# Hybrid attention and retention step: where three kinds of loads stand ahead of the output projection, and which half of a row block is turned first

## The chip, the cores and the metric

The kernel runs on one core of one Trainium2 chip. The metric is the device time in microseconds (us) of one execution. Several runs of the kernel are timed and their median is taken; one further execution is recorded by the hardware profiler, and all rows shown below come from that one.

## The reference, cut to what matters

One layer of a decoder with two groups of heads. 1024 prompt tokens and 32 sample tokens (8 sequences of 4) go through an input projection, a sparse softmax attention (A), a retention (B), and then through the part that this change is about, which the reference calls the merge:

```python
def _merge(x, oa, ob, ga, gb, p, w_out, g_post, w_ple_up, w_ple_gate):
    ya = silu(ga) * oa                        # attention, 512 columns
    yb = silu(gb) * head_norm(ob)             # retention, 512 columns
    y = concat([ya, yb]) @ w_out              # output projection, 1024 x 1024
    x = x + rmsnorm(y, g_post)                # post-norm with the weights g_post
    ple = p @ w_ple_up                        # the per-layer embedding, 256 -> 1024
    gate = sigmoid(x @ w_ple_gate)            # 1024 x 1024
    return x + ple * gate
```

All arrays are float32. The outputs are the new x of prompt and sample tokens, the new keys and values, and the retention's states.

## The kernel before, in words

**Products in three passes.** Every large product is done in a reduced-precision float32 format (F32R in the code), with each operand split into a high part and a low part: high times high, high times low, low times high. In the output projection these are the lines L262, L263 and L264 (`mm_a`): one row block of 128 tokens against 256 columns takes 8 slices of the contraction, three matmuls each, so 24 matmuls. Slices 0 to 3 belong to the attention's half of a row, slices 4 to 7 to the retention's half. The three matmuls of a slice, and the slices, run in order within a row block.

**Weights.** `load_w` (L173 to L177) brings 256 columns of a weight matrix in two halves of 512 rows through two buffers called `wraw`. ScalarE casts a half to the high part (L176), GpSimd subtracts to get the low part (L177). The 32 sample tokens use the raw weights directly (`mm_s`, L271), so a `wraw` buffer is free for the next column block only when the sample tokens' matmuls have read it.

**Attention phase.** It runs over 8 query blocks `qb`; SyncE's queue loads the queries of the next block (L1507) and the gates (L1536). Between the prompt's steps the sample tokens' attention is threaded in; GpSimd gathers its keys and values (L1144). Its last results go to `oaT` (L1379 and L1594), and from there to `ysT` (L1640), the left operand of `mm_s`. The attention's result of the prompt stands in `yaT`, 16 KB in each partition.

**The output projection's begin.** For each of the 8 row blocks `tb`, `split_T` makes the left operands `yTh` and `yTl`. The attention's half comes from `yaT`: a cast on ScalarE (L1619), a subtraction on GpSimd (L1620). The retention's half is loaded from DRAM as `yb` (three buffers, L1638), turned by four TensorE transposes into a PSUM bank called `pty` (L1624), cast on ScalarE (L1626), and subtracted on VectorE (L1627).

**The projection's loop.** Four column blocks `cb` of 256 columns; in each, eight row blocks and the sample tokens (called block 8), each into one of four PSUM banks. `take_y` empties a bank: ScalarE squares it for the norm (L1663), VectorE multiplies it by `gpost`, the post-norm weights spread over all partitions (L1664). While `cb` is 2, `load_p` brings the embedding's input `p` as `pv` (L1699), and ScalarE and VectorE split it (L1701, L1702). While `cb` is 3, `finish_y` completes the norm and turns the rows for the gate. Then come four column blocks of the gate (L262 to L264 into `pg`) and the embedding (`pu`), whose weights `load_up` brings (L1731).

**What sets the order.** Nothing is written out by hand: the program is traced in its textual order, and a scheduler fixes each engine's order of instructions at compile time by a simulated timeline, where earlier text has priority and an instruction that could start earlier may be pulled ahead. At run time each engine works through its fixed list, and waits at the head of the list when something is not ready. SyncE issues nearly all loads and stores, in one list.

**Memory.** Tiles of a later phase may stand where tiles of an earlier one stood; they wait for those to be released. In the compiled kernel before, `yaT` has the bytes 212960 to 229343 of each partition, and `gpost` the bytes 217056 to 221151, so `gpost` lies inside `yaT`. The pools on the right side are stacked from the top downwards.

## Time and profile before

| | |
|---|---|
| median of 3 runs | 1083.84 us (1078.32 to 1085.11) |
| the profiled execution's own time | 1081.17 us |
| its span, first to last instruction | 1079.4 us |
| time outside the span | 1.8 us |
| mean granted TensorE clock | 0.97 of full speed |
| TensorE matmul (PE) busy | 999.9 us, 93% of the span |
| VectorE (DVE) busy | 698.3 us, 65% |
| ScalarE (ACT) busy | 507.2 us, 47% |
| GpSimd (POOL) busy | 287.9 us, 27% |

How to read the rows: a row of the timeline has the start in us, the duration in us, the engine, the line of the program, the operation, what it writes and reads, and how many instructions the row merges; in brackets the idle time of the engine before it and what ended that. PEld is TensorE's loading of its stationary operand, SPq is SyncE's issue of a transfer. In a table by stretches each engine has its busy time and the number of instructions, then come the granted TensorE clock (1.00 is full speed), the mean busy share of the 16 DMA engines, and GB/s. A row of the waits has who waited for whom, the total in us, how often, and the longest. The chain of waits is followed back from the last instruction: each row is what the work then hung on.

### The profile page before, as it was taken

How to read it: one execution, taken by the hardware profiler on the slowest of the kernel's cores; microseconds unless marked ns; L12 is line 12 of the kernel's file. 1: busy time of each engine (PE TensorE's matmuls, PEld its weight loads, DVE VectorE, ACT ScalarE, POOL GpSimd, SP SyncE). 2: the span in 40 equal slices, each digit the busy share in tenths (PEclk: the TensorE clock that was granted, in tenths of full speed). 3: DMA queues.
4: the chain of work that ended last, by engine and by line, in shares of the span. 5: the costliest groups of instructions: out<-in, count | busy, mean ns of one | idle time of the engine just before them, and what ended most of it. 6: DMA issues, size and time to landing. Idle time of an engine off the chain costs nothing.

```text
span 1079.4 us, 19681 instructions
## 1 busy us (share of the span) xinstructions
PE 999.9 (93%) x7375; PEld 844.5 (78%) x7375; DVE 698.3 (65%) x2012; ACT 507.2 (47%) x1094; POOL 287.9 (27%) x287
## 2 busy tenths in 40 slices
PE   3899997988999889999889996999998799999998
PEld 2899997666776788898788884566665799999998
DVE  6847768989401898978967947776763522684332
ACT  5545554986434256842523436655554332452210
POOL 3102223111201532413713521635331321122100
PEclk9999999999999889999989995999999899999999
DMA  8211235546443211202201624524211511332211
GB/s 284 67 59 50 78 95 178 173 137 204 127 158 120 58 40 39 66 18 87 71 12 42 179 85 118 148 79 118 60 45 51 154 60 40 116 126 80 89 37 41
DMA packets 98309, 102.24 MB, mean 95 GB/s; under 512 B 21347, under 2 KB 88387, under 8 KB 95907
## 3 DMA queue, kind: packets, MB, share of 16 engines
q1 hardware_dynamic: 92450, 74.74, 23.1%
q0 software_dynamic: 5760, 26.22, 7.9%
q8 instruction: 58, 0.95, 0.4%
q14 instruction: 41, 0.33, 0.1%
HBM read 79.25 MB, written 21.68 MB: 94 GB/s over the span
## 4 chain that ended last, share of the span: by engine, by line
PE 65%; DVE 13%; issue 7%; ACT 6%; DMA 6%; POOL 3%; SPq 1%; DVEq 0%; POOLq 0%; ACTq 0%
PE pb L252 4%; PE pb L253 4%; PE pb L254 4%; PE pg L262 3%; PE pg L264 3%; PE pg L263 3%; PE po L262 2%; PE po L264 2%; PE po L263 2%; PE pvg L263 2%; PE pvg L264 2%; PE pvg L262 2%; PE ob L1577 2%; PE pox L808 2%; PE ptp L1569 2%
## 5 line engine op out<-in xcount | busy, mean ns | idle before, releaser
L1144 POOL DMA_INDIRECT kvs<-in_cache_kv,idx x64 | 66.1, 1032 | 92.0 <-ACT pT L1574 29.8
L262 PE MATMUL pqk<-whi_qkb,xh 128*128 128x256 f32 x256 | 75.7, 296 | 3.7 <-DVE rp L1033 3.7
L262 PE MATMUL po<-whi_o,yTh 128*128 128x256 f32 x256 | 74.0, 290 | 4.7 <-DVE x L1664 4.1
L262 PE MATMUL pvg<-whi_vgb,xh 128*128 128x256 f32 x256 | 76.6, 299 | 1.2 <-ACT sg L1046 1.1
L263 PE MATMUL pvg<-wlo_vgb,xh 128*128 128x256 f32 x256 | 75.9, 297 | 0.0
L264 PE MATMUL pvg<-whi_vgb,xl 128*128 128x256 f32 x256 | 74.6, 291 | 0.0
L263 PE MATMUL pqk<-wlo_qkb,xh 128*128 128x256 f32 x256 | 74.5, 291 | 0.0
L264 PE MATMUL pqk<-whi_qkb,xl 128*128 128x256 f32 x256 | 74.1, 289 | 0.0
L264 PE MATMUL po<-whi_o,yTl 128*128 128x256 f32 x256 | 73.3, 288 | 0.0
L263 PE MATMUL po<-wlo_o,yTh 128*128 128x256 f32 x256 | 73.1, 286 | 0.0
L262 PE MATMUL pg<-whi_g,yTh 128*128 128x256 f32 x256 | 72.7, 284 | 0.0
L264 PE MATMUL pg<-whi_g,yTl 128*128 128x256 f32 x256 | 72.3, 282 | 0.0
L263 PE MATMUL pg<-wlo_g,yTh 128*128 128x256 f32 x256 | 72.3, 282 | 0.0
L497 DVE SCALAR_TENSOR_TENSOR score<-r,wi,score 128x384 f32<-128x384 f32 (+5 forms) x42 | 44.3, 1054 | 21.0 <-ACT r L493 19.8
L1562 ACT ACTIVATE L<-L,mn 128x128 f32<-128x128 f32 (+7 forms) x64 | 49.5, 776 | 14.1 <-DVE mn L1559 13.9
L262 PEld LDWEIGHTS pqk<-whi_qkb,xh 128*128 128x128 f32 x256 | 49.3, 193 | 7.9 <-issue 5.0
L262 PEld LDWEIGHTS po<-whi_o,yTh 128*128 128x128 f32 x256 | 49.8, 194 | 6.4 <-DVE x L1664 4.3
L1758 DVE TENSOR_TENSOR sgm<-pu,sgm 128x256 f32<-128x256 f32 x32 | 13.6, 424 | 62.3 <-PE pu L264 55.3
L262 PEld LDWEIGHTS pvg<-whi_vgb,xh 128*128 128x128 f32 x256 | 49.7, 194 | 3.1 <-ACT sg L1046 1.3
L1569 PEld LDWEIGHTS ptp<-cst,L 128*128 128x128 f32 x288 | 31.9, 142 | 24.3 <-issue 19.6
L493 ACT ACTIVATE r<-si 128x384 f32<-128x384 f32 (+5 forms) x48 | 36.3, 759 | 30.2 <-PE si L351 29.0
L264 PEld LDWEIGHTS pqk<-whi_qkb,xl 128*128 128x128 f32 x256 | 49.5, 194 | 1.1 <-issue 0.8
(540 smaller groups left out, 3288.0 us busy)
## 6 DMA issues: line engine op xcount, KB each, us to landing
wraw_qkb<-in_w_in SPq DMA_DIRECT2D x16, 256.0 KB
wraw_vgb<-in_w_in SPq DMA_DIRECT2D x16, 256.0 KB
wraw_o<-in_w_out SPq DMA_DIRECT2D x8, 512.0 KB
qas<-qas_d SPq DMA_DIRECT2D x8, 512.0 KB
xr<-in_x_prompt SPq DMA_DIRECT2D x8, 512.0 KB
wraw_g<-in_w_ple_gate SPq DMA_DIRECT2D x8, 512.0 KB
out_y_prompt<-sgm SPq DMA_DIRECT2D x32, 128.0 KB
qas_d<-qst SPq DMA_DIRECT2D x8, 384.0 KB
```

The source lines that it names most:

```text
L252: nc.tensor.matmul(pt[:m, :n], wh, xh[:, k, ts], start=(k == 0), stop=False)
L253: nc.tensor.matmul(pt[:m, :n], wh, xl[:, k, ts], start=False, stop=False)
L254: nc.tensor.matmul(pt[:m, :n], wl, xh[:, k, ts], start=False, stop=(k == KC - 1))
L262: nc.tensor.matmul(pt[:, :n], ah, hi[:, k, :n], start=(k == 0), stop=False)
L263: nc.tensor.matmul(pt[:, :n], ah, lo[:, k, :n], start=False, stop=False)
L264: nc.tensor.matmul(pt[:, :n], al, hi[:, k, :n], start=False, stop=(k == kc - 1))
L493: nc.scalar.activation(r[:, :n], s[:, :n], AF.Relu)
L497: nc.vector.scalar_tensor_tensor(sc, r[:, :n], wi[:, qb, h:h + 1], sc, op0=ALU.mult, op1=ALU.add)
L808: nc.tensor.matmul(po[u2 * 64:u2 * 64 + 64, :], qbd[:, b, :], kT[:, u2 * 512:u2 * 512 + 512], start=True, stop=True)
L1144: return nc.gpsimd.indirect_dma_start(out=dst, out_offset=None, in_=kvflat, in_offset=bass.IndirectOffsetOnAxis(ap=idx, axis=0))
L1562: behind[0] = nc.scalar.activation(L[:, :n], L[:, :n], AF.Exp, bias=least, scale=-1.0, accum_out=sm[:, i4:i4 + 1])
L1569: nc.tensor.transpose(tp[:, i4 * 128:i4 * 128 + 128], P[i4][:, kb * 128:kb * 128 + 128], ident)
```

## The change

- `gpost` gets a pool of its own at the top of the right side, opened ahead of `yaT`, so that it stands beside `yaT` and not inside it; the other pools of the attention on the right side move down by 4096 bytes. It is loaded during the attention, in the query block `qb` 3, behind the load of the queries for block 4 (`issue_after` orders an instruction behind another one in the same engine's list).
- The loads of the embedding's input (`pv`) and of its weights (`wur`) are ordered behind the last weight load that was traced before them (`last_w`). For `pv` that is the second half of the projection's fourth column block, for the first `wur` the second half of the gate's first column block.
- `split_T` treats the retention's half of a row block first, then the attention's half, where it has both.
- In the first column block the sample tokens' product stands behind row block 3 instead of behind row block 2.

```diff
@@ load_w
+                last_w[0] = nc.sync.dma_start(raw[:, :, c:c + w], ...).ins
-                nc.sync.dma_start(raw[:, :, c:c + w], ...)
@@ ahead of yaT
+    gpp = ctx.enter_context(pool("gpp", side="right"))
+    gpost = gpp.tile([128, D], F32, name="gpost")
     yas = ExitStack()
     yap = yas.enter_context(pool("yap", side="right"))
     yaT = yap.tile([128, 4, T], F32, name="yaT")
@@ load_q
-        nc.sync.dma_start(q.bitcast(F32), qas_d[:, :, qb * 128:(qb + 1) * 128])
+        last_q[0] = nc.sync.dma_start(q.bitcast(F32), qas_d[:, :, qb * 128:(qb + 1) * 128]).ins
@@ for qb in range(8)
             qnext = load_q(qb + 1)
+            if qb == 3:
+                with tc.issue_after(last_q[0]):
+                    nc.sync.dma_start(gpost, I["g_post"].to_broadcast([128, D]))
@@ split_T
-        for a in range(2):
+        for a in (1, 0) if first is not None else range(2):
@@ behind the row blocks' split
-    gpost = mr.tile([128, D], F32, name="gpost")
-    nc.sync.dma_start(gpost, I["g_post"].to_broadcast([128, D]))
@@ load_p
-        nc.sync.dma_start(pv, src)
+        with tc.issue_after(last_w[0]):
+            nc.sync.dma_start(pv, src)
@@ for cb in range(4)
-        for tb in (8, *range(8)) if cb else (0, 1, 2, 8, 3, 4, 5, 6, 7):
+        for tb in (8, *range(8)) if cb else (0, 1, 2, 3, 8, 4, 5, 6, 7):
@@ load_up
-        nc.sync.dma_start(raw, w_up[:, cb * 256:(cb + 1) * 256].rearrange("(k p) c -> p k c", p=128))
+        with tc.issue_after(last_w[0]):
+            nc.sync.dma_start(raw, w_up[:, cb * 256:(cb + 1) * 256].rearrange("(k p) c -> p k c", p=128))
```

## The prediction, written before the change was run

> **What bounds the kernel now.** The page first: which engine is full. Then the stages of the output projection and what follows it, as a table by stretches.

> ```profile
> PE 999.9 (93%) x7375; PEld 844.5 (78%) x7375; DVE 698.3 (65%) x2012; ACT 507.2 (47%) x1094; POOL 287.9 (27%) x287
> ...
> 833.50:873.10 39.60, 31.80 (x248) 29.40 (x252) 20.18 (x36) 16.66 (x44) 16.15 (x11) 0.91 0.40 119
> 873.10:921.50 48.40, 48.40 (x419) 46.97 (x419) 10.13 (x24) 13.22 (x42) 9.52 (x4) 1.00 0.14 45
> 921.50:955.00 33.50, 32.12 (x289) 30.42 (x289) 28.13 (x90) 15.81 (x47) 4.82 (x2) 1.00 0.45 143
> 955.00:1079.40 124.40, 120.77 (x1035) 117.84 (x1033) 49.01 (x100) 27.97 (x59) 18.61 (x9) 1.00 0.20 67
> ```

> The rows are column block 0, blocks 1 and 2, block 3, and the gate. From 873.1 to the end TensorE is busy without a hole but for 1.4 us in block 3 and the last results. So a microsecond that TensorE gains ahead of 873 comes off the end one for one, as long as the weights keep up. Block 0 is the exception: 39.6 us, 31.8 busy, clock 0.91. TensorE's waits from there on name the 7.8 us:

> ```profile
> PE po L262 <- DVE x L1664: 4.1, 1, 4.1
> PE po L271 <- DVE ysT L1640: 2.3, 1, 2.3
> PE ptxs L1683 <- DVE rz_y L237: 1.4, 1, 1.4
> PE pty L1624 <- DMA yb<-yb_d: 1.3, 3, 0.6
> ```

> (1.4 is block 3's.) The chain of waits says what stood behind the longest:

> ```profile
> 846.07 1.47 DVE pTl L1702
> 847.56 0.37 SPq L1699
> ...
> 847.98 6.32 DMA gpost<-in_g_post
> ...
> 854.32 0.44 DVE x L1664
> ...
> 854.80 0.58 PE po L262
> 855.38 0.21 PE po L263
> ```

> SyncE issued `gpost` at 847.98, after a `pv` that waited for VectorE; it landed after 6.32 us; only then could VectorE empty a PSUM bank, and TensorE get the bank for row block 3. The DMA engines' share of the stretch, 0.40 against 0.14 in the next, is the crowd in front of it.

> The wait has a second price, the clock:

> ```profile
> 835.22:838.64 3.42, 1.61 (x17) 1.20 (x18) 1.72 (x2) 1.87 (x4) 3.42 (x4) 1.00 0.00 0
> 848.88:852.29 3.41, 1.34 (x11) 0.96 (x9) 0.90 (x2) 0.65 (x3) 0.00 (x0) 1.00 0.66 186
> 852.29:855.70 3.41, 0.90 (x4) 0.90 (x5) 1.80 (x5) 1.22 (x5) 0.00 (x0) 0.50 1.06 269
> 855.70:859.11 3.41, 3.41 (x19) 3.41 (x18) 0.73 (x2) 0.41 (x1) 0.00 (x0) 0.50 0.33 110
> ...
> 858.38 0.96 PE L1624 MATMUL pty<-cst,yb 128*128 128x128 f32 x4
> 859.09 0.38 PE L263 MATMUL po<-wlo_o,yTh 128*128 128x256 f32 x1
> ...
> 859.98 0.28 PE L262 MATMUL po<-whi_o,yTh 128*128 128x256 f32 x1
> 860.10 0.28 PE L263 MATMUL po<-wlo_o,yTh 128*128 128x256 f32 x1
> ```

> At half clock a matmul follows the last after 0.21 us, at full clock after 0.12 (859.98 to 860.10). A stretch of 3.4 us with 1.34 us of matmul was followed by half clock for 6.8 us; one with 1.61 us was not.

> **The change part by part.**

> *`gpost` early.* Its bytes lay inside `yaT`, so it could not land before `yaT` was read out, wherever it stood in SyncE's list; beside `yaT` it can. The load itself is the same, one issue of some 0.5 us. Gone: 4.14 us of wait (1). Also the half clock behind it (2): the 17 matmuls from 854.80 to 858.38 took 3.58 us and would take 17 x 0.12 = 2.04, and the four transposes from 858.38 to 859.09 took 0.71 and would take half; together 1.90 us. What is late next for the bank is ScalarE's square and VectorE's product, 0.4 us each, and the reading out of `yaT` for row blocks 1 and 2, whose `x2` tiles now lie in `yaT`'s bytes:

> ```profile
> 833.10 10.39 POOL L1620 TENSOR_TENSOR yTl<-yaT,yTh 128x512 fp32r<-128x512 f32 x8 [19.47 <-ACT yTh L1619]
> 833.25 1.39 DVE L1379 COPY oaT<-oT 64x8 f32<-64x8 f32 x8
> 834.68 1.08 DVE L1594 TENSOR_TENSOR oaT<-oaT,gaT 128x128 f32<-128x128 f32 x1
> 835.80 1.17 DVE L1640 COPY ysT<-oaT 128x128 f32<-128x128 f32 x1
> 834.42 0.28 PE L263 MATMUL po<-wlo_o,yTh 128*128 128x256 f32 x1
> 837.03 0.64 PE L271 MATMUL po<-wraw_o,ysT 128*32 128x256 f32 x8 [2.33 <-DVE ysT L1640]
> ```

> GpSimd is done with `yaT` at 843.5. Four banks hold four row blocks of 24 x 0.12 = 2.9 us, so the bank of row block 1 is wanted at about 833.5 + 4 x 2.9 = 845 at the earliest: covered, and without that cover it would cost what GpSimd is late.

> *Sample tokens behind row block 3.* Before, TensorE has six matmuls at 833.5 to 834.7 (high times high and high times low of three row blocks, each stopped at its low part from GpSimd) and then the sample tokens' product, which waits for VectorE's three steps until 837.0. Behind row block 3 that product is the fifth taker of four banks and cannot be pulled to this place before row block 0 is emptied. Row block 0's low part is there at 833.10 + 10.39 / 8 = 834.4, before the six matmuls end; after that GpSimd brings one per 1.3 us, and each frees 10 matmuls, 1.2 us. So of 2.33 us I take 2.0 (3); the ends are 0, if another waiting instruction stands in its place, and 2.33.

> *Retention's half first, `pv` and `wur` behind.* Three waits for `yb`, 1.33 us. `yb` was issued in between the `pv`, a `wur` and the `gpost`; without these 8 x 128 + 256 + 512 KB it lands sooner. Against it: row block 0's transposes take the bank that the sample tokens' last `oT` holds until VectorE's copies end at 834.6. I take 0.6 (4), ends -1.0 and 1.33.

> *Where `pv` goes.* Eight loads with a cast of 0.4 us on ScalarE and a subtraction of 0.4 to 1.6 us on VectorE move to blocks 2 and 3, behind the fourth block's weights:

> ```profile
> ACT pTh L1701 <- DMA pv<-in_p_T: 8.4, 4, 3.4
> ...
> 885.00:900.00 15.00, 15.00 (x133) 14.28 (x133) 3.25 (x8) 2.73 (x11) 0.00 (x0) 1.00 0.05 14
> 900.00:921.50 21.50, 21.50 (x182) 21.37 (x181) 3.51 (x9) 5.71 (x18) 4.76 (x2) 1.00 0.12 41
> ```

> There ScalarE and VectorE are about a fifth busy and the DMA engines at 0.05 to 0.12. ScalarE's waits for `pv` move too, 3.4 us at most, and the squares queue behind them; three banks in hand are 3 x 2.9 = 8.7 us. I take 0; ends -1.0 and 0. `wur` follows the gate's first weights and is used only in the gate's stretch: 0. In SyncE's list `pv` now stands behind the weights and ahead of the `xr` loads that block 3 wants.

> *`gpost`'s load in the attention.* Behind the queries of block 4. It shares the DMA engines with the gathers of the sample tokens' keys; TensorE has other work there: 0, ends -1.0 and 0.

> *The shift by 4096 bytes.* In the compiled kernel before, the first score tile `L` of the attention's second head group has the bytes 138464 to 142559, and the retention's result `acc` 132640 to 137247. Moved down by 4096, `L` lies on `acc`, and must wait until the last `acc` is stored:

> ```profile
> 620.25 2.93 DMA yb_d<-acc
> ...
> 663.10 6.50 SPq L1097 DMA_DIRECT2D yb_d<-acc  x2
> ...
> 668.97 0.28 DVE L1096 TENSOR_TENSOR acc<-acc,sgs 32x128 f32<-32x128 f32 x1 [0.48 <-ACT acc L1091]
> ...
> 669.51 0.27 DVE L1559 CUSTOM_DVE_ANT_0 L<-sa,near 128x128 f32<-128x128 f32 x1
> ```

> The last store of `acc` is issued at about 669.3; another one held its taker for 2.93 us. `L` was written at 669.51. If the store lands at once, nothing moves; with 2.93 us `L` moves to 672.2, by 2.7 us. VectorE, ScalarE's exponentials and TensorE queue behind it. The store is the sample tokens' alone, 16 KB, so I take the nearer third, -1.0 (5); ends 0 and -2.7.

> Sum: 4.14 + 1.90 + 2.0 + 0.6 - 1.0 = 7.6 us. From the profiled execution's 1081.17 that is 1073.5; that execution lies 2.7 us under the median of the runs, 1083.84, and from the median it is 1076.2. I predict the middle, **1075**.

> [...] The row: half clock began at 852.29, when TensorE had stood still for 1.6 us, after a stretch with 1.34 us of matmul in it. [...]

> **The rivals**, each from the middle of the two bases, 1082.5.

> 1. *The half clock stays* (by what another stall does): 7.6 - 1.9 = 5.7 off, 1077. For: any new hole that leaves about 1.3 us of matmul in 3.4 us brings it back. Against: none of the remaining waits is longer than 0.6 us in the sum above. 0.08.

> 2. *The first 10 us only change their waits.* Terms (3) and (4) come to nothing, since TensorE's fixed order puts transposes that wait for `oT`'s bank, or the low parts from GpSimd, where the sample product stood; and (5) takes 2.7: 4.14 + 1.90 - 2.7 = 3.3 off, 1079. For: the order is fixed ahead of time, and before it put the sample product 2.3 us too early. Against: the low parts come from GpSimd every 1.3 us from 834.4 on, which is about TensorE's own pace. 0.19.

> 3. *The second block's weights come late, and it ends slower.* The sample tokens' product frees `wraw`, and it moves back:

> ```profile
> 863.17 0.64 PE L271 MATMUL po<-wraw_o,ysT 128*32 128x256 f32 x8
> ...
> 863.87 0.38 SPq L173 DMA_DIRECT2D wraw_o<-in_w_out  x1
> ...
> 867.25 1.05 ACT L176 CAST whi_o<-wraw_o 128x1024 fp32r<-128x1024 f32 x1 [0.17 <-DMA wraw_o<-in_w_out]
> ...
> 868.38 2.40 POOL L177 TENSOR_TENSOR wlo_o<-wraw_o,whi_o 128x1024 fp32r<-128x1024 f32 x1 [21.13 <-ACT whi_o L176]
> ```

> From the product to the finished low part it is 870.8 - 863.2 = 7.6 us, and block 1 begins at 873.1. If both halves of the product are put within 7.6 us of block 0's end, TensorE waits: at worst both halves at the very end, 7.6 + 2.4 for the second subtraction = 10.0 us, and 1.9 for the half clock. 7.6 - 11.9 = -4.3: slower, 1087. Against: behind row block 3 there are four more, 11.5 us, and `yb` of the sample tokens is no longer held up. 0.06.

> 4. *All of it comes, and nothing is paid for the shift:* 4.14 + 1.90 + 2.33 + 1.33 = 9.7 off, 1073. 0.11.

> **How the numbers follow.** The forecast has 0.56, the rivals 0.08, 0.19, 0.06 and 0.11. The range: the low end is rival 4 from the fastest run shown, 1078.3 - 9.7 = 1068.6; the high end takes in rival 2 and the open ends of the small terms, 1083. Outside are most of rival 3 and some of the tails. One per cent, 10.8 us, is about what a measurement of this kernel can tell from no change; from 1083.84 that is below 1073.0 and above 1094.7. Below lie half of rival 4 and, since the bases differ by 2.7 us, some two fifths of the forecast: 0.28. Above lies none of the cases at its price, only rival 3 with more than one block's weights late: 0.04. Within: 0.68.

> **What would show it.** Right: no wait of TensorE for `x` at L1664 in block 0; clock 1.00 throughout; the sample product no longer in the first 5 us; block 0 at 30 to 33 us instead of 39.6; `pv` casts behind the fourth block's weights, and blocks 1 to 3 still full. (5) shows as VectorE's first `L` of the second head group waiting for the store of `acc`. Wrong: TensorE waiting at block 1's begin for `wraw_o` or `wlo_o` (rival 3), a row of half clock in block 0 (1), new waits on `yTl`, `pty` or `oT` of 2 us or more (2), or an attention that ends later than 833 by over 3 us.

## The result, and the profile after

The changed kernel takes 1071.88 us (median of 7 runs, 1065.73 to 1074.34) against 1083.84 for the kernel before: a ratio of **0.9901** (95% interval 0.9878 to 0.9924), 10.7 us less by the ratio (12.0 between the medians). In the later series of runs below, where the kernel before takes 1086.68 us, the ratio was 0.9901 again (0.9862 to 0.9940). The forecast was 1075; the time lies in its range, 3 us below it. That closeness hides errors of 5.0, 2.8 and 1.6 us, of both signs, as the runs below show.

The profiled execution of after is the fastest of its runs, 1065.73 us (span 1063.9). Of the 15.4 us between the two profiled executions 4.1 lie ahead of the attention, where the engines' instructions stand in the same order in both: that is the spread between runs, not the change. So the comparison goes by stages: the attention (first `sa` matmul to first `po`), column block 0 (to the sample tokens' first matmul of block 1), blocks 1 to 3 (to their first matmul of the gate), the gate (to the start of the last matmul). Tables by stretches, before and then after, the columns being length, the busy times of PE, PEld, VectorE, ScalarE and GpSimd, clock, DMA share and GB/s:

```profile
655.96:833.48 177.52, 167.45 (x1229) 107.59 (x1229) 117.97 (x438) 103.30 (x236) 65.95 (x65) 0.95 0.30 86
833.48:873.05 39.57, 31.76 (x245) 29.37 (x245) 20.20 (x36) 16.68 (x44) 16.17 (x11) 0.91 0.40 119
873.05:952.22 79.17, 77.79 (x673) 75.43 (x673) 35.48 (x104) 27.61 (x84) 14.34 (x6) 1.00 0.25 81
952.22:1075.49 123.27, 123.27 (x1065) 119.78 (x1064) 50.94 (x108) 29.39 (x63) 18.61 (x9) 1.00 0.22 71
```

```profile
651.86:825.49 173.63, 165.00 (x1229) 105.82 (x1229) 120.22 (x438) 100.46 (x233) 64.22 (x65) 0.94 0.31 90
825.49:854.86 29.37, 28.58 (x245) 27.34 (x245) 11.64 (x28) 14.11 (x35) 14.75 (x10) 1.00 0.34 106
854.86:934.38 79.52, 77.99 (x673) 75.45 (x673) 41.25 (x110) 30.30 (x93) 16.73 (x7) 1.00 0.31 97
934.38:1060.04 125.66, 123.41 (x1065) 119.75 (x1064) 53.41 (x110) 29.64 (x64) 20.47 (x9) 1.00 0.21 70
```

Block 0 is 10.2 us shorter, and its clock is full. The attention is 3.9 shorter, which the prediction had at 1 us longer. The gate is 2.4 longer, which it had at nothing. TensorE's waits in after, from block 0 to the end, show what is left (who waited for whom, total, times, longest):

```profile
PE pty L1634 <- DVE x L1684: 2.2, 1, 2.2
PE ptxs L1691 <- DVE ry_y L238: 1.1, 1, 1.1
PE pty L1634 <- issue: 0.8, 1, 0.8
PE po L265 <- DVE yaT L1598: 0.4, 1, 0.4
PE pty L1634 <- DVE ry_y L238: 0.4, 1, 0.4
```

No wait for `x` at L1672 (the old L1664), none for `ysT`, none for `yb`. (Lines of after are 3 to 10 higher than before.) The wait of 2.2 us for `x` at L1684 is new. SyncE's issues in after show the three moved loads:

```profile
683.95 0.65 SPq L1542 DMA_DIRECT2D gpost<-in_g_post  x1
...
880.79 17.66 SPq L1708 DMA_DIRECT2D pv<-in_p_T  x8
904.04 0.93 SPq L175 DMA_DIRECT2D wraw_g<-in_w_ple_gate  x2
905.02 0.50 SPq L1741 DMA_DIRECT2D wur<-in_w_ple_up  x1
```

### The profile page after: what moved, and what is told of

It is laid out like the page before. It is cut to its first block, busy times and chain, and to the rows that moved or that the text cites. A ratio compares the mean times of both kernels' runs of the same rounds, so it can differ in the third digit from the quotient of the medians.

```text
span 1063.9 us, 19686 instructions
## 1 busy us (share of the span) xinstructions
PE 991.7 (93%) x7375; PEld 838.6 (79%) x7375; DVE 699.8 (66%) x2012; ACT 504.2 (47%) x1092; POOL 288.1 (27%) x287
## 4 chain that ended last, share of the span: by engine, by line
PE 53%; DVE 8%; ACT 2%; DMA 2%; issue 1%; POOL 1%; SPq 0%; DVEq 0%; ACTq 0%; POOLq 0%
PE ob L1587 4%; PE ptp L1579 4%; PE pg L265 3%; PE pg L267 3%; PE pg L266 3%; PE po L265 3%; PE po L266 2%; PE po L267 2%; PE pvg L265 2%; PE pvg L266 2%; PE pvg L267 2%; PE sa L1563 2%; PE sa L1564 2%; PE pqk L265 2%; PE pqk L266 1%; PE pqk L267 1%
## 5 line engine op out<-in xcount | busy, mean ns | idle before, releaser
L1147 POOL DMA_INDIRECT kvs<-in_cache_kv,idx x64 | 63.6, 994 | 84.1 <-ACT pT L1584 44.7
L1572 ACT ACTIVATE L<-L,mn 128x128 f32<-128x128 f32 (+7 forms) x64 | 49.5, 775 | 13.7 <-DVE mn L1569 13.6
L266 PEld LDWEIGHTS pvg<-wlo_vgb,xh 128*128 128x128 f32 x256 | 50.7, 198 | 0.5
L267 PEld LDWEIGHTS pvg<-whi_vgb,xl 128*128 128x128 f32 x256 | 50.6, 198 | 0.6
```

The source lines that it names most:

```text
L266: nc.tensor.matmul(pt[:, :n], ah, lo[:, k, :n], start=False, stop=False)
L267: nc.tensor.matmul(pt[:, :n], al, hi[:, k, :n], start=False, stop=(k == kc - 1))
L1147: return nc.gpsimd.indirect_dma_start(out=dst, out_offset=None, in_=kvflat, in_offset=bass.IndirectOffsetOnAxis(ap=idx, axis=0))
L1572: behind[0] = nc.scalar.activation(L[:, :n], L[:, :n], AF.Exp, bias=least, scale=-1.0, accum_out=sm[:, i4:i4 + 1])
```

## The experiments

**The theory** that these tables led to had three parts: the 4096 bytes change the attention's order, and that makes it shorter; block 0 gains by `gpost` and by the begin's new order, each for its own wait; and the gate loses by `wur` being late. Its rivals: the attention's difference is chance; the queue alone carries block 0. Times are on one chip for each group of runs; the stage lengths come from one profiled execution of each kernel, between the borders above. "Old" and "new" are the two orders that the attention has in the compiled kernels: in the four profiles of the old order every engine goes through the same list of instructions, in the ten of the new through another one, and the two part at TensorE's 13th matmul.

| kernel | attention | block 0 | blocks 1-3 | gate | ratio to before |
|---|---|---|---|---|---|
| before | old 177.5 | 39.6 | 79.2 | 123.3 | |
| before_again | old 183.5 | 40.3 | 80.8 | 124.3 | |
| queue_only | old 183.5 | 34.1 | 79.0 | 126.6 | 0.9986 (0.9964 to 1.0007) |
| rest_only | old 185.8 | 30.7 | 79.6 | 128.2 | 0.9956 (0.9935 to 0.9978) |
| shift_only | new 178.1 | 39.1 | 79.4 | 124.6 | 0.9951 (0.9928 to 0.9973) |
| gpost_only | new 178.0 | 34.1 | 81.0 | 124.3 | 0.9934 (0.9908 to 0.9960) |
| gpost_pv | new 179.4 | 33.0 | 80.7 | 123.3 | 0.9911 (0.9884 to 0.9937) |
| no_queue | new 178.0 | 30.8 | 80.9 | 124.7 | 0.9894 (0.9862 to 0.9926) |
| no_halves | new 180.3 | 28.9 | 80.8 | 123.6 | 0.9879 (0.9846 to 0.9913) |
| pv_queued | new 181.6 | 29.4 | 79.3 | 124.3 | 0.9864 (0.9830 to 0.9898) |
| old_halves | new 179.5 | 28.9 | 79.6 | 125.4 | 0.9877 (0.9843 to 0.9911) |
| old_sample | new 179.6 | 29.4 | 78.9 | 126.5 | 0.9877 (0.9845 to 0.9909) |
| after | new 173.6 | 29.4 | 79.5 | 125.7 | 0.9901 (0.9878 to 0.9924) |
| after_again | new 177.8 | 29.4 | 80.0 | 128.4 | 0.9901 (0.9862 to 0.9940) |

### The shift alone

```diff
+    gpp = ctx.enter_context(pool("gpp", side="right"))
+    gpad = gpp.tile([128, D], F32, name="gpad")
+    nc.gpsimd.memset(gpad[:, 0:1], 0.0)
     yas = ExitStack()
     yap = yas.enter_context(pool("yap", side="right"))
```

> The kernel before with 4096 unused bytes ahead of yaT's pool, nothing else: gpost is loaded in its old place, block 0 begins as before. The trace of after holds ScalarE's table loads at 16 where before has 18, and its attention (first sa of the first query block to the first matmul of the output projection) takes 173.6 us where before takes 177.5. Theory: the order that the 4096 bytes force (the samples' normalisation ahead of the first exponentials) is the cause, so this kernel shows the short attention too: 16 table loads, 173 to 175 us from first sa to first po, none of the three waits for the gathered keys (1.6 us before); block 0 as before, 38 to 41 us with gpost's wait in it; time 3 to 4 us below before, ratio 0.9965. Rival A, the prediction's term (5): the shift costs 1 us, ratio 1.001, attention 178 to 179. Rival B: the two attentions differ from run to run or by gpost's load in it: attention 177 to 178, ratio 1.000.

The bytes of `gpad` are not used. This kernel has the new order, so the 4096 bytes cause it. By the time the theory holds: 0.9951, 4.5 us between the medians, and the prediction's own term, 1 us slower, is outside the interval. By the stage it does not: 178.1 us is what the rivals said (178 to 179 and 177 to 178), and the 173.6 of after was luck. Both are true if the old order takes longer than 177.5 us in other runs, so the kernel before was profiled once more:

> The kernel before once more, for a second look at its attention. Its first profile has 177.5 us from first sa to first po, as the kernels with the shifted order have (178.0, 178.0, 178.0, and 173.6 in after), yet by the times the shift alone is 0.5% faster. Theory (the old order has more holes and falls into half clock more easily): this attention is longer than 178.5 us, as the one other kernel with the old order showed (185.8). Rival: 177 to 178 us, and the shift's gain lies elsewhere or is none.

183.5 us, and the two other kernels with the old order show 183.5 and 185.8. The mean of the four is 182.6 us, that of the ten profiles with the new order 178.6 (173.6 to 181.6). The difference, 4.0 us, is near that of shift_only's time, 4.5 (1083.03 against 1087.52). The two sets of profiles overlap, so the time is the firmer of the two.

What changed in the order shows in ScalarE's timeline. Before loads an activation table three times around the first exponentials:

```profile
662.56 1.28 ACT L1562 ACT_TABLE_LOAD   x1
663.86 0.40 ACT L1562 ACTIVATE L<-L,mn 128x128 f32<-128x128 f32 x1
...
665.53 1.28 ACT L1081 ACT_TABLE_LOAD   x1
666.82 0.20 ACT L1081 ACTIVATE gy<-gv 32x2 f32<-32x2 f32 x1
...
668.95 1.28 ACT L1562 ACT_TABLE_LOAD   x1
```

In after the samples' normalisation (`gy`) and the last product into `acc` stand ahead of the first `L`. (That the scheduler does so because `L` has to wait for the bytes of `acc` is argued, not shown.)

```profile
658.48 0.20 ACT L1084 ACTIVATE gy<-gv 32x2 f32<-32x2 f32 x1
659.82 0.77 ACT L1094 ACTIVATE acc<-acc,gz,gy 32x64 f32<-32x64 f32 x2 [1.15 <-DVE gz L1090]
661.31 1.28 ACT L1572 ACT_TABLE_LOAD   x1 [0.72 <-DVE mn L1569]
662.61 0.40 ACT L1572 ACTIVATE L<-L,mn 128x128 f32<-128x128 f32 x1
```

Two loads fewer, 2 x 1.28 = 2.56 us of ScalarE. Over the whole span it is 18 of them in before and 16 in after, of 1283 ns each.

But the loads that fell away aren't the gain. Here is TensorE alone, before and then after, cut where the ninth `ob` matmul starts; the columns are length, busy time, clock, DMA share and GB/s:

```profile
655.96:679.99 24.03, 16.87 (x89) 0.61 0.35 98
679.99:833.48 153.49, 150.58 (x1141) 1.00 0.30 84
```

```profile
651.86:675.97 24.11, 15.90 (x89) 0.60 0.34 98
675.97:825.49 149.52, 149.10 (x1141) 1.00 0.30 88
```

The table loads that differ all lie in the first stretch, and it isn't shorter. In it the new order has a longer wait of TensorE for VectorE's `mn`, again before and then after:

```profile
659.70 0.47 PE L1553 MATMUL sa<-kahi,qas 128*128 128x128 f32 x1 [2.20 <-DVE mn L1559]
```

```profile
661.29 0.48 PE L1563 MATMUL sa<-kahi,qas 128*128 128x128 f32 x1 [7.89 <-DVE mn L1569]
```

And yet both orders have done the same number of matmuls when the stretch ends, 23.7 to 24.2 us after the first `sa` in all fourteen profiles. The whole difference arises after that.

Part of that shows in the clock. All profiles begin the attention with half clock (0.50) until 17 to 20 us after the first `sa` (18.8 in before, 19.4 in after). More half clock follows, from 10 to 14 us later on, in three of the four profiles with the old order (6.8, 6.8 and 10.2 us of it, 3.4 of the last another 48 us on) and in four of the ten with the new (3.4, 3.4, 3.4 and 6.8). The stretches around it in queue_only (length, busy times, clock, DMA share, GB/s), and TensorE's wait inside:

```profile
679.97:683.38 3.41, 1.55 (x11) 1.05 (x9) 0.50 (x4) 0.71 (x2) 2.31 (x3) 1.00 0.72 223
683.38:686.79 3.41, 1.08 (x4) 0.67 (x6) 2.21 (x12) 2.25 (x6) 1.10 (x2) 0.50 0.13 38
686.79:690.21 3.42, 3.42 (x18) 1.87 (x18) 2.66 (x9) 0.72 (x4) 0.79 (x1) 0.50 0.26 77
```

```profile
682.86 0.33 PE L1324 MATMUL pkg<-cst,kvs 128*128 128x128 f32 x1 [1.67 <-issue]
685.71 0.66 PE L1556 MATMUL sa<-kahi,qas 128*128 128x384 f32 x1 [2.53 <-DVE mn L1562]
```

From the granted 0.50 the estimate is that half clock for 6.8 us costs up to 3.4; in block 0 the same 245 matmuls kept TensorE busy for 31.76 us with 6.8 us of it (before) and for 28.58 without (after). Averaged, that is 3.0 us in the old order (23.8 / 4 / 2) and 0.9 in the new (17.0 / 10 / 2): at most some 2 of the 4 us. TensorE's waits behind the ninth `ob` are 4.8 us on average in the old order and 3.5 in the new, 1.2 more; in after there are none, which is its luck, and before has 2.2. Why the new order waits less there is not shown.

### gpost alone, the rest alone

gpost_only takes the pool `gpp`, `last_q` and the early load from the change, nothing else. rest_only takes all of the change but these.

```diff
# rest_only against after
-    gpp = ctx.enter_context(pool("gpp", side="right"))
-    gpost = gpp.tile([128, D], F32, name="gpost")
...
-            if qb == 3:
-                with tc.issue_after(last_q[0]):
-                    nc.sync.dma_start(gpost, I["g_post"].to_broadcast([128, D]))
...
+    gpost = mr.tile([128, D], F32, name="gpost")
+    nc.sync.dma_start(gpost, I["g_post"].to_broadcast([128, D]))
```

> Only the first part of the change: gpost in a pool of its own, loaded behind the fourth block's queries; embedding's loads, the halves' order and the sample tokens' place as before. Theory: it has the short attention (173 to 175 us) and loses gpost's 4.1 us and the half clock behind it (1.9), but keeps the waits for ysT (2.3) and yb (1.3): block 0 33 to 35 us instead of 39.6, clock 1.00 in it, nothing lost in the gate; 9 to 10 us below before, ratio 0.991. Rival: the crowd of pv loads in front of the bank matters more than gpost, and block 0 stays at 37 us or more; 4 to 5 us below before, ratio 0.996.

> The change without its first part: gpost in yaT's bytes and in its old place, the rest (embedding's loads behind the last weights', retention's halves first, sample tokens behind row block 3) as after. Theory: attention as before, 177 to 178 us with 18 table loads; gpost still has to wait until yaT is read out, at about 10 us into block 0, and lands some 2 to 3 us later, since the loads in front of it are gone: a wait for x of 1 to 4 us stays in block 0, which takes 32 to 37 us; the gate's begin loses 2.7 us as in after; in sum 0 to 5 us below before, ratio 0.9975. Rival: the queue's order is the whole gain of block 0: 29.4 us as in after, ratio 0.993.

The first came as the theory said in block 0, 34.1 us, but for the clock: behind the wait for `ysT` it was half for 3.4 us, and for 3.4 more in block 3, which may be why the time, 0.9934, gained less. The second came near its rival in block 0: 30.7 us. Alone, `gpost` brings 5.5 us of block 0's 10.2, the rest 8.9; together 10.2, not 14.4. **The parts remove the same wait.** TensorE's waits in block 0 of rest_only:

```profile
PE po L274 <- DVE x L1669: 1.2, 1, 1.2
PE pty L1629 <- issue: 0.8, 1, 0.8
PE po L265 <- DVE yaT L1593: 0.5, 1, 0.5
```

`gpost` comes from its old place, issued 13.1 us into block 0 (14.5 before), and yet the wait for `x` is down from 4.1 to 1.2 us: the first row block is emptied 17.5 us into block 0 instead of 20.8. Of its 8.9 us the time shows 4.8 (1082.75 against 1087.52); its gate is longer, 128.2 us against 123.3.

### The queue

```diff
# queue_only against before
+    last_w = [None]
...
-                nc.sync.dma_start(raw[:, :, c:c + w], ...)
+                last_w[0] = nc.sync.dma_start(raw[:, :, c:c + w], ...).ins
...
+        with tc.issue_after(last_w[0]):
             nc.sync.dma_start(pv, src)
...
+        with tc.issue_after(last_w[0]):
             nc.sync.dma_start(raw, w_up[...])
```

> Before with only pv and wur put behind the last weights; gpost in its old place, the halves' order and the sample tokens' place as before. Theory: the crowd ahead of gpost was most of its wait, so this part alone takes block 0 from 39.6 to 33 to 35 us: the wait for x falls from 4.1 to 1 to 2 us with no half clock behind it, while the wait for ysT (2.3 us) stays, because the product still stands among the first matmuls; the gate loses 2 to 4 us as in after; attention of the old order, 177 to 186 us. Ratio 0.9975. Rival: gpost still lands late, since it cannot be issued before yaT is read out, and block 0 stays at 37 us or more, ratio 1.001.

Block 0 34.1 us as the theory has it, but not as it came there. TensorE's waits in block 0 of queue_only are these two only:

```profile
PE po L274 <- DVE ysT L1643: 2.3, 1, 2.3
PE po L265 <- DVE yaT L1591: 0.5, 1, 0.5
```

With `gpost` where it always was, nothing waits for it: SyncE issues it 12.0 us into block 0 (849.59) instead of 14.5 (847.98 before), and the first row block is emptied at 853.6. The half clock of block 0 stands now behind the wait for `ysT` (840 to 847). The longer gate, 126.6 us, takes 3.3 of the 5.5 us back, and by the time alone no gain is shown: the interval of 0.9986 takes in 1.

> The change without its second part: pv and wur free to be issued early, the rest as after. Theory: with gpost landed in the attention and the halves turned, the early loads hold nobody up: short attention (173 to 175 us), block 0 29 to 31.5 us, and the gate's order is that of before, without after's waits of 2.2 and 1.1 us there; 12 to 14 us below before, ratio 0.988, some 2 us faster than the whole change. Rival: the early pv, with casts and subtractions among the begin's work, cost what the change took them away for: a wait for yb or for a bank of 2 us or more, block 0 32 us or more, ratio 0.991 or above.

no_queue takes `issue_after` away from `pv` and `wur` in the change. Block 0 is 30.8, as the theory has it, but with a wait for `yb` of 1.3 us, and the ratio lies between the theory and the rival. So the queue's part is worth 1.5 us of block 0 where the other parts are there, and 5.5 where they are not. At 0.9894 the whole is about what the change is, not 2 us faster.

### The begin's order

```diff
# old_halves, and with it no_halves and gpost_pv
-        for a in (1, 0) if first is not None else range(2):
+        for a in range(2):
# old_sample, and with it gpost_pv
-        for tb in (8, *range(8)) if cb else (0, 1, 2, 3, 8, 4, 5, 6, 7):
+        for tb in (8, *range(8)) if cb else (0, 1, 2, 8, 3, 4, 5, 6, 7):
```

> The whole change, but with each row block's attention half handled first and the retention half second, as before. Theory (the prediction's term 4): with embedding's loads gone from the front of the queue, yb is there in time in either order, and the order of the halves is worth 0 to 1 us: block 0 29 to 30.5 us, ratio 0.990. Rival: the transposes are TensorE's only work while GpSimd brings the first low parts, and without them at the front TensorE waits for yTl: block 0 31 us or more, ratio 0.992.

> The whole change, but with the sample tokens' product behind row block 2 as before. Theory (the prediction's term 3): the product stands where it waits for VectorE's ysT, or holds a bank that the next row block wants; block 0 31 to 32 us instead of 29.4, with a wait for ysT of up to 2.4 us or of one for a bank; ratio 0.9915. Rival: once the transposes of retention's half stand among the first matmuls, the product behind row block 2 finds ysT done: block 0 29.4 to 30 us, ratio 0.990.

Each undone alone costs nothing: 28.9 and 29.4 us. For old_sample that is the rival, against the theory. Undone together:

> Before with two things only: gpost early in its own pool, and pv (not wur) behind the last weights; halves and sample tokens as before. Undoing either the halves' order or the sample tokens' place cost nothing (block 0 28.9 and 29.4 us); here both are undone. Theory: one of them is needed, because with both undone the product stands among the first matmuls again and waits 2.3 us for ysT: block 0 31.5 to 33.5 us, ratio 0.990. Rival: neither is needed: 29 to 30 us, ratio 0.987.

33.0 us; one of the two is needed. The waits in block 0 of gpost_pv:

```profile
PE po L274 <- DVE ysT L1650: 2.4, 1, 2.4
PE po L265 <- DVE yaT L1598: 0.4, 1, 0.4
```

Against no_halves, which differs only in the sample tokens' place, that is 33.0 - 28.9 = 4.1 us: the wait for `ysT`, 2.4, and 1.7 by the half clock of 3.4 us behind it (TensorE busy for 30.57 us against 28.87). Turning retention's half first costs 0.5 us by comparison (pv_queued 29.4, no_halves 28.9): no_halves has no wait for `pty` at all, after has one of 0.8.

### The gate

> The whole change, but for wur, which is free to be issued early as before; only pv stands behind the last weights. Theory: after's lost time in the gate (TensorE's waits of 2.2, 1.1 and 0.4 us at its begin, gate 125.7 us from its first matmul to the last against 123.3 before) comes from wur being ready late and in an order of VectorE's that puts two gated sums ahead of the last row block's residual; with wur early the gate has the order of before: 123.3 to 125 us, while block 0 keeps after's 29.4 to 30 us. 1 to 2 us faster than the whole change, ratio 0.988. Rival: wur's load and its cast crowd block 0's begin as pv's did: block 0 30.8 us or more and nothing is gained, ratio 0.990 or above.

The gate is 124.3 us, block 0 29.4: as expected. Over all profiles the gate splits by `wur` alone: 125.4 to 128.4 us in the six profiles in which `wur` stands behind the last weights, 123.3 to 124.7 in the eight in which it does not; means 126.8 and 124.0. (Two of the six, those of rest_only and after_again, have 3.4 us of half clock in the gate, which costs some 1.8: TensorE is busy there for 125.20 us in after_again, and for 123.41 in after.) Part of this comes back one stage earlier: five of the eight have 3.4 us of half clock in block 3, and none of the six, so that blocks 1 to 3 take 80.3 us on average in the eight and 79.4 in the six. With both stages a late `wur` costs 1.9 us. VectorE's timeline at the gate's begin in after, and TensorE's wait:

```profile
942.27 1.58 DVE L1768 TENSOR_TENSOR sgm<-sh_u,sgm 32x256 f32<-32x256 f32 x1
943.78 0.14 DVE L242 TENSOR_TENSOR ry_y<-ry_y,rz_y 128x1 f32<-128x1 f32 x1
943.85 2.95 DVE L1769 TENSOR_TENSOR sgm<-sgm,x 128x256 f32<-128x256 f32 x2
946.73 1.27 DVE L1684 SCALAR_TENSOR_TENSOR x<-x,ry_y,xr 128x1024 f32<-128x1024 f32 x1
```

```profile
948.14 1.06 PE L1634 MATMUL pty<-cst,x 128*128 128x128 f32 x8 [2.25 <-DVE x L1684]
```

The last row block's residual `x` stands behind a product and two sums of the gate, and TensorE's transposes wait for it. In before it stands ahead of them, and the same sample-token product takes 0.41 us instead of 1.58 (see VectorE beside GpSimd at the end):

```profile
958.33 1.29 DVE L1676 SCALAR_TENSOR_TENSOR x<-x,ry_y,xr 128x1024 f32<-128x1024 f32 x1
...
966.06 0.41 DVE L1758 TENSOR_TENSOR sgm<-sh_u,sgm 32x256 f32<-32x256 f32 x1
```

Why the scheduler orders them so when `wur` comes late was not tried.

### Put together

no_halves is the change without the halves' turn, with only `pv` behind the last weights; after_again ran beside it.

> The combination that the runs point to: gpost early, pv (not wur) behind the last weights, sample tokens behind row block 3, the halves' order as before. Expected: block 0 28.9 to 29.4 us, gate 123.3 to 124.5 us instead of after's 125.7, attention 173 to 181 us; ratio 0.9865, 2 us faster than the whole change. Rival: the two do not add up, the gate loses the 2 us again and the ratio is 0.990.

> The whole change once more, on the chip of the runs above and for a second profile of its attention. Theory: ratio 0.988 to 0.991 as at first; attention nearer to the 178 to 181 us of the other kernels with the same order than to the 173.6 us of its first profile; block 0 29.4, gate 125.4 to 126.5 us with the waits of 2.2 and 1.1 us at its begin. Rival: the whole change's attention has something that the others lack: 173 to 175 us again.

1073.41 us against 1077.33 for the whole change on the same chip. Block 0 and gate are as expected (28.9 and 123.6). The ratios to before, 0.9879 and 0.9901, have intervals that overlap, so that it is faster isn't shown by the times. By the stages it gains 0.5 us in block 0 and 2 to 5 in the gate, and loses 1 in blocks 1 to 3 (80.8 against 79.5 and 80.0). after_again's attention, 177.8, is the theory's.

## Why the prediction was right, and where it was not

- **Terms 1 and 2, `gpost` and the clock behind it.** Right that both go. The half clock was too small: counted over 21 instructions it came to 1.90 us, but for the same 245 matmuls block 0's busy time fell from 31.76 to 28.58, by 3.2; what else ran in the two stretches of half clock was left out.
- **Terms 3 and 4, `ysT` and `yb`.** The waits went (2.33 and 1.33; predicted 2.0 and 0.6), so block 0 gained 10.2 where the sum had 4.14 + 1.90 + 2.0 + 0.6 = 8.6; the 1.6 are 1.3 of the clock, 0.3 and 0.7 of these two, less the new wait of 0.8 for `pty`. But the assignment to parts of the change failed. The wait for `yb` went with `pv`, and the turned halves cost 0.5; the sample tokens' place and the halves replace one another; and rest_only shows that most of the wait for `x` would have gone with `gpost` where it was. The sum adds waits, and waits are right to add; it would have been wrong to add what each edit saves.
- **Term 5, the shift: wrong in sign.** The step priced a wait put into the old order. The compiled kernel has another order from there on, and the wait that the prediction named as its sign doesn't show: in after VectorE writes the first `L` at 660.94, right behind the last product into `acc`, and the second head group's first `L` at 663.50, right behind `near`, 11.6 us after the first `sa` instead of 13.6. TensorE does wait 5.7 us longer at the begin, but has caught up 24 us after the first `sa`. In sum -4.0 us in the attention instead of +1.0. This is the largest error, 5 us.
- **`wur` at 0: wrong.** "Used only in the gate's stretch" is true, and it costs 2.8 us there by the order at the gate's begin (1.9 with what blocks 1 to 3 give back). `pv` at 0 holds: blocks 1 to 3 take 79.5 against 79.2 us. So does `gpost`'s load in the attention: with it nine profiles show 173.6 to 181.6 us, without it shift_only 178.1.
- **The sum.** 10.2 + 4.0 - 2.8 = 11.4 us (12.3 with 1.9 for `wur`) against the forecast's 7.6 and the measured 10.7 (8.2 to 13.2 by the interval). That is on the border between within 1% (given 0.68) and faster (0.28); with the sign of term 5 right the second would have had most of it.
- **Rivals.** No half clock and no new wait of 2 us in block 0 (1 and 2). The second block's weights were in time (3), by little: GpSimd's second subtraction ended at 847.54 + 4.78 = 852.32, and block 1 began at 854.86.

```profile
847.54 4.78 POOL L180 TENSOR_TENSOR wlo_o<-wraw_o,whi_o 128x1024 fp32r<-128x1024 f32 x2 [8.74 <-ACT whi_o L179]
```

Rival 4 named the begin best: all of it came and no price was paid for the shift.

## What to carry to other kernels

Edits that take away one wait are not a sum: run each alone and undo each alone, since here `gpost` alone brought 5.5 us and the rest alone 8.9 of 10.2, while of the smaller parts one cost 0.5 us and one 1.9. Where a scheduler fixes the order, a tile moved by a few KB or a load moved behind another is a new order somewhere far from the edit; compare the compiled order of each engine before pricing the move as a wait. A stage of 180 us whose clock may halve was 8 us apart between profiles of one order (177.5 and 185.8 us); several kernels that share a stage are as many samples of it.

## What the runs showed of the hardware

**VectorE beside GpSimd.** The product of 32 x 256 elements at 942.27 took 1.58 us while GpSimd worked, and 0.41 in before, where GpSimd's row had ended at 965.65. The two profiles hold it four times each: 0.41 us in all 3 cases without a GpSimd instruction beside it, 1.58 to 1.72 us in all 5 with one. GpSimd's rows in after and in before:

```profile
941.18 5.01 POOL L180 TENSOR_TENSOR wlo_g<-wraw_g,whi_g 128x1024 fp32r<-128x1024 f32 x2 [24.91 <-ACT whi_g L179]
```

```profile
964.18 1.47 POOL L1733 TENSOR_TENSOR wul<-wur,wuh 128x512 fp32r<-128x512 f32 x1
```
